# Hybrid decoder layer: key operands, head scaling and score sign between VectorE and ScalarE, and convolution steps over two PSUM banks

## The chip, the cores and the metric

One core of a Trainium2 chip runs the whole layer. The metric is the device time of one execution in microseconds; the time of the kernel before is the median of three runs, 1490.66 us (1486.98 to 1492.48). About 0.5% of it, 7.5 us, is what a measurement of this kernel can tell from no change.

## The reference, cut to what matters

One layer is computed for a prompt of 16 + 1024 rows and for 8 sample rows with a cache of 4096 past positions each. Everything is fp32.

```python
proj = rms_norm(x, ln_mix_pre) @ w_in               # q, k, v (512 each), a, g (512 each)
u = a * sigmoid(g)
s = q.k / 8 - slope[h] * (q_pos - k_pos), masked to k_pos <= q_pos   # 4 heads, 2 maps each
a = softmax(s0) - lam * softmax(s1);  o = a @ v
attn = rms_norm(o, subln) * (1 - 0.2)               # over the head's 128 values
y = causal depthwise convolution of u, width 31, + bias
conv = silu(layer_norm(y))                          # over 512 channels
x = x + rms_norm(concat(attn, conv) @ w_out, ln_mix_post)
out = x + rms_norm((silu(h @ w_gate) * (h @ w_up)) @ w_down, ln_ffn_post),  h = rms_norm(x, ln_ffn_pre)
```

## The kernel before, in words

Each fp32 matrix product on TensorE is made of three products of rounded halves (an operand's high part H in fp32r, and the rest L): H.H, H.L and L.H, in `mm3` (L146 to L149). The stages are these, in the order of the program:

- Projections. `stripe_ag(ct)` makes u for 128 channels (four of them, ct = 0 to 3), `stripe_v`, `stripe_q`, `stripe_k` make a head's values, queries and keys, each in three chunks of 280, 384 and 384 columns.
- Keys. For each chunk and each of a head's two maps `stripe_k` (L296 to L299) builds two operands of 128 partitions: R1 holds the map's 64 key rows rounded, twice (in both halves of the partitions), and R2 the remainder k - R1, twice. R1's own half is copied by ScalarE and the other by VectorE; R2's own half is subtracted by GpSimd and the other by VectorE. L1 of the queries has the rounded query in one half and its remainder in the other, so that two matmuls (L502 with R1, L503 with R2) give the scores to full precision.
- Convolution. `conv_half(ct, half)` does 31 taps over 512 columns: the first 11 go as products by ScalarE (L406, L408) and sums by GpSimd (L409) into an SBUF buffer, the other 20 by VectorE into a PSUM tile of one bank (`pcv`, two of them): L410, then L418 nineteen times, with the SBUF sum added before the last (L416). The last step writes into u. There are eight halves; their instructions are planned behind others (`high_priority(offset=-400)`).
- Attention, `attn(h, i)`: 32 units of 128 query rows, W = 144 to 1040 keys. For each map: matmuls into PSUM pieces (`ps1`), one VectorE instruction for each piece that adds the distances, scales, writes p and keeps the running maximum (L504), then for both maps the negated maximum nm (L510), the exponentials by ScalarE with their sums (L512), the factor cc (L514, L516), the combination of both maps (L520), transposes, and the product with the values (L542). After every fourth unit the head's output is scaled: copy and sums of squares by ScalarE (L550, L552), two small steps t by VectorE (L556, L557), a power by GpSimd (L559), a scaling by VectorE (L561), and two units later (`head_out`) the transposes and a copy by ScalarE (L571).
- The sample rows' attention over the cache is spread over the rest of the program by `dec_step`: the products of pages of keys with the query by GpSimd (L677, 128 of them), their sums by VectorE (L687).
- Output projection and FFN (`c_block`, `ffn`): matmuls into `ps1` tiles (mo, pg, pu, dn), emptied by VectorE and ScalarE (L907, L967, L972, L996).

Tiles of PSUM have a name and a number of buffers: `ps1` has six (`ns=6`), `pb` three, `pcv` two, `po1` and `pdec` one each. That is more than the eight banks; the framework's planner places tiles whose lives don't overlap into the same bank. It also orders each engine's instructions by a simulation of the program with its own costs, so that an edit can move instructions far from it. Each engine then runs its own list in that order. The pages' DMAs are issued from SP's queue.

Of the kernel before, what the change touches and what calls it, by code (L numbers as in the profile page):

```python
# [8 lines left out]
F32 = mybir.dt.float32  # L9
# [3 lines left out]
ALU = mybir.AluOpType  # L13
# [28 lines left out]
SLAB = 1056  # L42


@with_exitstack
def tile_layer(ctx: ExitStack, tc: tile.TileContext, I, O, cfg):
# [61 lines left out]
    subln = cst.tile([P, P], F32, name="subln")  # L108
    convb = cst.tile([P, 4], F32, name="convb")
# [174 lines left out]
    def stripe_k(h):  # L284
# [111 lines left out]
    def conv_half(ct, half):  # L396
        ut = u[ct]
        a = 512 * half
        acc = pcv(f"acc{ct}{half}")
        n = cfg["taps"]  # L400
        if n:
            if not convbuf:
                convbuf.extend(kv(f"cb{i}") for i in range(2))
            cb = convbuf[half]
            accp, t = cb[:, 0:512], cb[:, 512:1024]
            S.activation(accp, ut[:, a : a + 512], AF.Identity, scale=cw[:, ct, 0:1], bias=convb[:, ct : ct + 1])  # L406
            for k in range(1, n):
                S.mul(t, ut[:, a + k : a + k + 512], cw[:, ct, k : k + 1])  # L408
                G.tensor_tensor(accp, accp, t, op=ALU.add)  # L409
            V.tensor_scalar(acc, ut[:, a + n : a + n + 512], cw[:, ct, n : n + 1], None, op0=ALU.mult)  # L410
        else:
            V.tensor_scalar(acc, ut[:, a : a + 512], cw[:, ct, 0:1], convb[:, ct : ct + 1], op0=ALU.mult, op1=ALU.add)
        for k in range(max(n, 0) + 1, CW):
            src = ut[:, a + k : a + k + 512]
            if n and k == CW - 1:
# [65 lines left out]
    def attn(h, i):  # L481
        W = META + P * (i + 1)
        qs = slice(i * P, (i + 1) * P)
        if i == 0:
            att_st["l"] = smt(f"l{h}", 16, 2)
            att_st["ssq"] = smt(f"ssq{h}", 8, 2)
            if h == 0:
                att_st["junk"] = smt("junk", P, 1)
# [58 lines left out]
        if i % 4 == 3:  # L547
            oh = att(f"oh{h}{i}")
            b0 = i - 3
            S.copy(oh, o)  # L550
            for b in range(4):
                S.activation(att_st["junk"], oh[:, b * P : (b + 1) * P], AF.Square, accum_out=ssq[:, b0 + b : b0 + b + 1])  # L552
            bs = slice(b0, i + 1)
            l0 = lh.rearrange("p (i j) -> p i j", j=2)[:, bs, 0]
            t1 = smt(f"t1{h}{i}", 4)
# [3 lines left out]
            G.tensor_tensor(r, t1, mhalf[:, :4], op=ALU.pow)  # L559
            for b in range(4):  # L560
                V.scalar_tensor_tensor(  # L561
                    oh[:, b * P : (b + 1) * P], oh[:, b * P : (b + 1) * P], r[:, b : b + 1], subln,
                    op0=ALU.mult, op1=ALU.mult,
                )

            def head_out():
                pt = pb(f"oT{h}{i}")
                for b in range(4):
                    T.transpose(out=pt[:, b * P : (b + 1) * P], in_=oh[:, b * P : (b + 1) * P], identity=ident)
                m = att(f"mo{h}{i}")  # L570
                S.copy(m, pt)  # L571
# [697 lines left out]
    for ct in range(4):  # L1269
# [111 lines left out]
    nb=3, no=1, ns=6, nd=1, nc=2,  # L1381
# [50 lines left out]
```

## Time and profile before

| | |
|---|---|
| median of 3 runs | 1490.66 us |
| the profiled execution, its own time | 1491.31 us |
| its span | 1489.3 us |
| TensorE (PE) busy | 1375.3 us, 92% |
| VectorE (DVE) busy | 964.9 us, 65% |
| GpSimd (POOL) busy | 562.6 us, 38% |
| ScalarE (ACT) busy | 514.8 us, 35% |
| DMA | 264.35 MB, mean 178 GB/s |

The stages in the trace, in us from the span's start: the first loads to 40; projections of a and g, with the convolution beside them, to 135; attention and the remaining projections to 515, with the convolution to 227; output projection and FFN to the end. An instruction's duration on DVE includes time in which it has begun and waits for something that is not a semaphore. A busy PE is not PE at its peak, since matmuls overlap.

### The profile page before, as it was taken

The page shows a single profiled execution, that of the slowest core. Times are in us where ns is not written, and L with a number is a line of the kernel's source. Part 1 is how long each engine was busy: PE and PEld are TensorE (multiplying, and loading weights), DVE is VectorE, ACT ScalarE, POOL GpSimd, SP SyncE. Part 2 cuts the span into 40 slices and gives each one's busy share as a digit, 9 for nine tenths or more (in the row PEclk, how much of TensorE's full clock was granted, in tenths as well). Part 3 has the DMA queues.
Part 4 walks back from the last instruction along what each step waited for, and adds up shares of the span by engine and source line. Part 5 has one row for each costly group of instructions (what it writes and reads, how often), then busy time and mean ns, then how long its engine had stood idle before and what let it go on. Part 6 is the DMA issues. An engine that isn't in the chain of part 4 may idle for free.

```text
span 1489.3 us, 21639 instructions
## 1 busy us (share of the span) xinstructions
PE 1375.3 (92%) x6960; PEld 1071.5 (72%) x6960; DVE 964.9 (65%) x1531; ACT 514.8 (35%) x1021; POOL 562.6 (38%) x351
## 2 busy tenths in 40 slices
PE   6999678888875899999999999999999999999997
PEld 6999678877864778777776776767676666566666
DVE  5689998894888456855665747575654176353158
ACT  6566565547555324511312012211112112112122
POOL 3698663542425211363554445455540000000014
PEclk9999899998886899999999999999999999999999
DMA  8211012422424554768886777677676735763454
GB/s 263 72 44 45 15 44 93 121 85 92 156 81 148 181 173 136 268 214 255 278 267 208 250 244 246 235 258 267 216 253 225 260 122 192 261 192 124 162 182 173
DMA packets 199534, 264.35 MB, mean 178 GB/s; under 512 B 16279, under 2 KB 99672, under 8 KB 199413
## 3 DMA queue, kind: packets, MB, share of 16 engines
q1 hardware_dynamic: 188768, 254.40, 52.2%
q10 hardware_dynamic: 10653, 8.57, 1.8%
q8 instruction: 55, 0.90, 0.2%
q14 instruction: 58, 0.48, 0.1%
HBM read 245.92 MB, written 17.48 MB: 177 GB/s over the span
## 4 chain that ended last, share of the span: by engine, by line
PE 68%; DVE 16%; issue 5%; DMA 4%; ACT 3%; SPq 2%; POOL 1%; DVEq 0%; POOLq 0%; ACTq 0%
PE pg L147 6%; PE pg L148 6%; PE pg L149 6%; PE pu L147 5%; PE pu L148 5%; PE pu L149 5%; PE dn L147 5%; PE dn L148 5%; PE dn L149 5%; PE pv L729 4%; DVE p L504 2%; PE mo L149 2%; PE mo L147 2%; PE mo L148 2%; DVE acc L418 2%
## 5 line engine op out<-in xcount | busy, mean ns | idle before, releaser
L677 POOL TENSOR_TENSOR k<-k,qB 128x1024 f32<-128x1024 f32 x128 | 320.5, 2518 | 269.1 <-DMA k<-in_cache_k 227.6
L687 DVE TENSOR_REDUCE s<-k 128x16 f32<-128x1024 f32 x128 | 154.8, 1212 | 99.8 <-POOL k L677 95.0
L953 ACT CAST wH<-wr 128x1024 fp32r<-128x1024 f32 x66 | 69.0, 1048 | 251.9 <-DVE wL L955 148.9
L147 PE MATMUL dn<-wH,aH 128*128 128x512 f32 x352 | 141.6, 406 | 4.2 <-DVE y L996 2.6
L147 PE MATMUL pu<-hH,wH 128*128 128x512 f32 x352 | 141.0, 401 | 1.3 <-DVE y L996 1.3
L149 PE MATMUL pu<-hH,wL 128*128 128x512 f32 x352 | 139.7, 398 | 1.5 <-DVE sm2n_t L121 1.5
L148 PE MATMUL dn<-wL,aH 128*128 128x512 f32 x352 | 140.9, 400 | 0.0
L148 PE MATMUL pu<-hL,wH 128*128 128x512 f32 x352 | 140.1, 399 | 0.0
L147 PE MATMUL pg<-hH,wH 128*128 128x512 f32 x352 | 140.1, 398 | 0.0
L149 PE MATMUL dn<-wH,aL 128*128 128x512 f32 x352 | 140.0, 398 | 0.0
L148 PE MATMUL pg<-hL,wH 128*128 128x512 f32 x352 | 139.6, 396 | 0.0
L149 PE MATMUL pg<-hH,wL 128*128 128x512 f32 x352 | 139.5, 396 | 0.0
L955 DVE TENSOR_TENSOR wL<-wr,wH 128x1024 fp32r<-128x1024 f32 x66 | 104.4, 1582 | 43.8 <-ACT wH L953 23.6
L996 DVE TENSOR_TENSOR y<-dn,y 128x512 f32<-128x512 f32 x144 | 95.0, 682 | 33.7 <-PE dn L149 33.4
L409 POOL TENSOR_TENSOR cb<-cb 128x512 f32<-128x512 f32 x80 | 103.6, 1325 | 26.5 <-ACT cb L408 14.2
L418 DVE SCALAR_TENSOR_TENSOR acc<-u,cw,acc 128x512 f32<-128x512 f32 x144 | 99.5, 748 | 0.3
L1068 POOL TENSOR_TENSOR y<-y,wfpost 128x512 f32<-128x512 f32 x10 | 17.3, 1747 | 207.1 <-ACT ft L1066 207.0
L147 PEld LDWEIGHTS dn<-wH,aH 128*128 128x128 f32 x352 | 67.6, 192 | 30.7 <-issue 6.9
L147 PEld LDWEIGHTS pu<-hH,wH 128*128 128x128 f32 x352 | 66.6, 189 | 28.8 <-issue 12.0
L148 PEld LDWEIGHTS dn<-wL,aH 128*128 128x128 f32 x352 | 67.2, 191 | 24.4 <-issue 10.3
L147 PEld LDWEIGHTS pg<-hH,wH 128*128 128x128 f32 x352 | 66.2, 188 | 24.9 <-issue 9.0
L148 PEld LDWEIGHTS pu<-hL,wH 128*128 128x128 f32 x352 | 66.5, 189 | 24.2 <-issue 10.3
(582 smaller groups left out, 2986.5 us busy)
## 6 DMA issues: line engine op xcount, KB each, us to landing
k<-in_cache_k SPq DMA_DIRECT2D x256, 256.0 KB
v<-in_cache_v SPq DMA_DIRECT2D x256, 256.0 KB
wr<-in_w_gate SPq DMA_DIRECT2D x22, 512.0 KB
wr<-in_w_up SPq DMA_DIRECT2D x22, 512.0 KB
wr<-in_w_down SPq DMA_DIRECT2D x22, 512.0 KB
sd<-in_w_down SPq DMA_DIRECT2D x22, 512.0 KB
sw_gate<-in_w_gate SPq DMA_DIRECT2D x20, 512.0 KB
sw_up<-in_w_up SPq DMA_DIRECT2D x20, 512.0 KB
```

Of the source, the lines that this page charges most:

```text
L147: T.matmul(out, lhsT=wH, rhs=xH, start=first, stop=False)
L148: T.matmul(out, lhsT=wH, rhs=xL, start=False, stop=False)
L149: mark(T.matmul(out, lhsT=wL, rhs=xH, start=False, stop=last))
L409: G.tensor_tensor(accp, accp, t, op=ALU.add)
L418: V.scalar_tensor_tensor(dst, src, cw[:, ct, k : k + 1], acc, op0=ALU.mult, op1=ALU.add)
L504: V.tensor_tensor_reduce(out=p[:, a:e], in0=o, in1=bias[:, b0 + a : b0 + e], scale=SLOPES[h], scalar=NEG if a == 0 else mx[:, j : j + 1], ...
L677: x = G.tensor_tensor(kt, kt, qB.unsqueeze(1).to_broadcast([P, 2, 512]), op=ALU.mult)
L687: x = V.tensor_reduce(s.rearrange("p a c -> p (a c)"), kt.rearrange("p a (c d) -> p (a c) d", d=HD), axis=AX.X, op=ALU.add)
L729: x = T.matmul(pv[32 * g : 32 * g + 8, :], lhsT=a[:, q + i, :], rhs=vt[:, i, :], start=q + i < 4, stop=q + i >= NPG - 4, tile_position=(0, ...
L953: S.copy(H[:, :1024], raw[:, :1024])
L955: V.tensor_tensor(L[:, :1024], raw[:, :1024], H[:, :1024].bitcast(F32), op=ALU.subtract)
L996: V.tensor_tensor(y[b][:, ws], o, y[b][:, ws], op=ALU.add)
```

## The change

- In `stripe_k` the other half of R1 and the other half of R2 are copied by ScalarE (the latter from R2's own half); R2's own half stays with GpSimd.
- The scores are negated: L504 scales by the negative slope and keeps a minimum, which is nm itself; L510 is gone, and the exponential has a scale of -1.
- cc is made by `tensor_scalar` with two per-partition operands in place of `scalar_tensor_tensor`.
- A head's output: the epsilon goes in as one more column of the squares (l0 times a constant, column 129 of each block in a tile of its own tag, `oh`), so that t is gone; the scaling by r is done by ScalarE, and subln is applied with a per-partition factor (`sublnT`, a new DMA of 128 values and one ScalarE step at the start) in the copy after the transposes.
- The convolution runs over 1024 columns in one PSUM tile of two banks, one buffer; ScalarE's first step covers 1024 columns, the other products and sums stay at 512, in two halves of one buffer.
- `ns` goes from 6 to 4.

```diff
+    sublnT = cst.tile([P, 1], F32, name="sublnT")
...
                 S.copy(R1s[j][sl, d], k[sl, d])
-                V.tensor_copy(R1s[j][ot, d], k[sl, d])
-                (G if cfg["r2_g"] else V).tensor_tensor(R2s[j][sl, d], k[sl, d], R1s[j][sl, d].bitcast(F32), op=ALU.subtract)
-                V.tensor_tensor(R2s[j][ot, d], k[sl, d], R1s[j][sl, d].bitcast(F32), op=ALU.subtract)
+                S.copy(R1s[j][ot, d], k[sl, d])
+                G.tensor_tensor(R2s[j][sl, d], k[sl, d], R1s[j][sl, d].bitcast(F32), op=ALU.subtract)
+                S.copy(R2s[j][ot, d], R2s[j][sl, d].bitcast(F32))
...
+            D.dma_start(sublnT, I["subln_w"][0].rearrange("(p o) -> p o", o=1))
+        S.mul(sublnT, sublnT, (1.0 - LAM_INIT) * P ** 0.5)
...
+        acc = ps.tile([P, SEQ], F32, tag="c", name=f"acc{ct}", bufs=1)
...
+        S.activation(accp, ut[:, 0:SEQ], AF.Identity, scale=w(0), bias=convb[:, ct : ct + 1])
+        for k in range(1, n):
+            for a in (0, 512):
+                S.mul(t[:, a : a + 512], ut[:, a + k : a + k + 512], w(k))
+            for a in (0, 512):
+                G.tensor_tensor(accp[:, a : a + 512], accp[:, a : a + 512], t[:, a : a + 512], op=ALU.add)
+        V.tensor_scalar(acc, ut[:, n : n + SEQ], w(n), None, op0=ALU.mult)
+        for k in range(n + 1, CW):
+            src = ut[:, k : k + SEQ]
+            if k == CW - 1:
                 V.tensor_tensor(acc, acc, accp, op=ALU.add)
+            V.scalar_tensor_tensor(acc if k < CW - 1 else src, src, w(k), acc, op0=ALU.mult, op1=ALU.add)
...
-                    out=p[:, a:e], in0=o, in1=bias[:, b0 + a : b0 + e], scale=SLOPES[h],
-                    scalar=NEG if a == 0 else mx[:, j : j + 1], op0=ALU.add, op1=ALU.max, accum_out=mx[:, j : j + 1],
+                    out=p[:, a:e], in0=o, in1=bias[:, b0 + a : b0 + e], scale=-SLOPES[h],
+                    scalar=-NEG if a == 0 else nm[:, j : j + 1], op0=ALU.add, op1=ALU.min, accum_out=nm[:, j : j + 1],
...
-        V.tensor_scalar(nm, mx, -1.0, None, op0=ALU.mult)
...
-        V.scalar_tensor_tensor(cc, lh[:, 2 * i : 2 * i + 1], neglam, rl, op0=ALU.mult, op1=ALU.mult)
+        V.tensor_scalar(cc, lh[:, 2 * i : 2 * i + 1], neglam, rl, op0=ALU.mult, op1=ALU.mult)
...
-            V.scalar_tensor_tensor(t1, l0, EPS, l0, op0=ALU.mult, op1=ALU.mult)
-            V.scalar_tensor_tensor(t1, ssq[:, bs], 1.0 / P, t1, op0=ALU.mult, op1=ALU.add)
+            S.mul(ov[:, :, P], l0, (P * EPS) ** 0.5)
+            for b in range(4):
+                S.activation(att_st["junk"], ov[:, b, : P + 1], AF.Square, accum_out=ssq[:, b0 + b : b0 + b + 1])
...
-                V.scalar_tensor_tensor(
-                    oh[:, b * P : (b + 1) * P], oh[:, b * P : (b + 1) * P], r[:, b : b + 1], subln,
-                    op0=ALU.mult, op1=ALU.mult,
-                )
+                S.mul(ov[:, b, :P], ov[:, b, :P], r[:, b : b + 1])
...
-                S.copy(m, pt)
+                S.mul(m, pt, sublnT)
...
-    nb=3, no=1, ns=6, nd=1, nc=2,
+    nb=3, no=1, ns=4, nd=1, nc=2,
```

## Rows read from the trace of the kernel before

**Rows 1.** The page's first part: busy us, share of the span, instructions
```profile
PE 1375.3 (92%) x6960; PEld 1071.5 (72%) x6960; DVE 964.9 (65%) x1531; ACT 514.8 (35%) x1021; POOL 562.6 (38%) x351
```

**Rows 2.** Stretches: PE, PEld, DVE, ACT, POOL busy (count), granted clock, DMA share, GB/s
```profile
40.00:135.00 95.00, 95.00 (x601) 92.94 (x601) 77.74 (x125) 55.44 (x89) 73.21 (x59) 1.00 0.13 38
135.00:240.00 105.00, 81.82 (x473) 76.87 (x472) 102.41 (x192) 60.07 (x132) 64.40 (x47) 0.89 0.16 48
240.00:320.00 80.00, 72.16 (x486) 68.15 (x485) 70.01 (x161) 49.37 (x142) 35.72 (x25) 1.00 0.32 97
320.00:400.00 80.00, 62.90 (x392) 59.82 (x391) 56.46 (x103) 48.41 (x112) 30.69 (x18) 0.85 0.40 129
400.00:515.00 115.00, 84.85 (x461) 73.29 (x461) 85.59 (x202) 56.24 (x146) 47.23 (x28) 0.81 0.38 125
515.00:1489.00 974.00, 952.12 (x4400) 675.29 (x4398) 550.81 (x695) 217.62 (x356) 294.50 (x146) 0.99 0.66 218
```

**Rows 3.** The chain of waits from 135 to 515 us, shares by engine and line
```profile
by line: issue 11.5%; DVE p L504 8.2%; DVE acc L418 7.8%; DVE p L520 6.1%; DVE R L299 5.0%; DVE R L297 4.4%; PE o L542 3.9%; ACT p L512 3.7%; DVE cc L516 3.4%; DVE oh L561 2.4%; DVE nm L510 2.4%; DVE s L687 2.2%; PE AT L528 1.9%; DVE L L268
```

**Rows 4.** Groups of DVE from 135 to 515: count, busy us, mean ns, idle before
```profile
L418 DVE SCALAR_TENSOR_TENSOR acc<-u,cw,acc 128x512 f32<-128x512 f32 x59 | 42.0, 745 | 0.2
...
L299 DVE TENSOR_TENSOR R<-kT,R 64x384 fp32r<-64x384 f32 (+1 forms) x24 | 22.7, 946 | 0.7
L516 DVE SCALAR_TENSOR_TENSOR cc<-l,neglam,rl 128x1 f32<-128x1 f32 x32 | 20.2, 631 | 0.3
L297 DVE CAST R<-kT 64x384 fp32r<-64x384 f32 (+1 forms) x24 | 19.5, 817 | 0.6
L561 DVE SCALAR_TENSOR_TENSOR oh<-oh,or,subln 128x128 f32<-128x128 f32 x32 | 16.7, 583 | 2.4 <-POOL or L559 2.3
L510 DVE TENSOR_SCALAR nm<-mx 128x2 f32<-128x2 f32 x32 | 16.7, 525 | 0.3
L557 DVE SCALAR_TENSOR_TENSOR t<-ssq,t 128x4 f32<-128x4 f32 x8 | 5.4, 674 | 12.9 <-ACT junk L552 12.9
L556 DVE SCALAR_TENSOR_TENSOR t<-l 128x4 f32<-128x4 f32 x8 | 4.5, 558 | 2.6 <-ACT p L512 2.6
```

**Rows 5.** Single lines of the kernel: duration ns min/median/max, first and last start
```profile
L510 DVE TENSOR_SCALAR nm<-mx x32: 149/170/2379, 166.9 to 476.7; 128x2 f32<-128x2 f32 x32
...
L121 DVE TENSOR_SCALAR hr_t<-hs x8: 135/154/155, 515.9 to 603.2; 128x1 f32<-128x1 f32 x8
```

**Rows 6.** Timeline of DVE and POOL in the last head: start us, us, what
```profile
460.88 2.36 POOL L138 TENSOR_TENSOR wo3L<-wo3r,wo3H 128x1024 fp32r<-128x1024 f32 x1 [1.82 <-ACT wo3H L136]
461.09 2.17 DVE L516 SCALAR_TENSOR_TENSOR cc<-l,neglam,rl 128x1 f32<-128x1 f32 x1
...
463.29 1.03 DVE L520 SCALAR_TENSOR_TENSOR p<-p,cc,p 128x400 f32<-128x400 f32 x2
```

**Rows 7.** Timeline of three convolution steps, then DVE's 1024-column step of L911
```profile
192.49 2.06 DVE L418 SCALAR_TENSOR_TENSOR acc<-u,cw,acc 128x512 f32<-128x512 f32 x3
...
L911 DVE SCALAR_TENSOR_TENSOR xr<-z,zr_r,xr x8: 1278/1284/1286, 513.4 to 597.9; 128x1024 f32<-128x1024 f32 x8
```

**Rows 8.** Groups of ACT from 135 to 515
```profile
L296 ACT CAST R<-kT 64x384 fp32r<-64x384 f32 (+1 forms) x24 | 11.3, 480 | 0.5
...
L436 ACT ACTIVATE u<-yT,ln2n,ln_r 128x128 f32<-128x128 f32 x4 | 1.7, 467 | 6.7 <-DVE ln2n L427 6.7
```

**Rows 9.** Who waited for whom: us in total, times, longest; 110 to 515, then 515 on
```profile
ACT p L512 <- DVE nm L510: 43.4, 20, 9.4
...
POOL k L677 <- DMA k<-in_cache_k: 26.5, 2, 21.1
...
DVE s L687 <- POOL k L677: 90.7, 35, 6.6
...
DVE s L709 <- POOL dg L704: 40.6, 7, 7.0
```

**Rows 10.** The page's group of L996: count, busy us, mean ns, idle before
```profile
L996 DVE TENSOR_TENSOR y<-dn,y 128x512 f32<-128x512 f32 x144 | 95.0, 682 | 33.7 <-PE dn L149 33.4
```

More of the change, by code (lines that the diff above doesn't have):

```diff
@@ L42 @@
 SLAB = 1056
+OHW = P + 4
 @with_exitstack
@@ L368, in att_consts @@
         V.tensor_scalar(subln, subln, 1.0 - LAM_INIT, None, op0=ALU.mult)
+        with nc.allow_non_contiguous_dma("128 values, once"):
+            D.dma_start(sublnT, I["subln_w"][0].rearrange("(p o) -> p o", o=1))
+        S.mul(sublnT, sublnT, (1.0 - LAM_INIT) * P ** 0.5)
         D.dma_start(pts, I["page_table"].rearrange("(o b) n -> o (b n)", o=1))
@@ L394, in tile_layer, with conv @@
     convbuf = []
-    def conv_half(ct, half):
+    def conv(ct):
         ut = u[ct]
-        a = 512 * half
-        acc = pcv(f"acc{ct}{half}")
+        acc = ps.tile([P, SEQ], F32, tag="c", name=f"acc{ct}", bufs=1)
         n = cfg["taps"]
[L401 to L415, printed above, removed]
+        if not convbuf:
+            convbuf.extend(kv(f"cb{i}") for i in range(2))
+        accp, t = convbuf
+        w = lambda k: cw[:, ct, k : k + 1]
+        S.activation(accp, ut[:, 0:SEQ], AF.Identity, scale=w(0), bias=convb[:, ct : ct + 1])
[8 more added lines that the diff above has]
+            if k == CW - 1:
                 V.tensor_tensor(acc, acc, accp, op=ALU.add)
-            dst = acc if k < CW - 1 else src
-            V.scalar_tensor_tensor(dst, src, cw[:, ct, k : k + 1], acc, op0=ALU.mult, op1=ALU.add)
+            V.scalar_tensor_tensor(acc if k < CW - 1 else src, src, w(k), acc, op0=ALU.mult, op1=ALU.add)
     def ln_stats(src, rows, name):
@@ L487, in attn @@
             if h == 0:
-                att_st["junk"] = smt("junk", P, 1)
+                att_st["junk"] = smt("junk", P + 1, 1)
         lh, ssq = att_st["l"], att_st["ssq"]
@@ L495, in attn @@
         pj = []
-        mx = smt(f"mx{h}{i}", 2, 4)
+        nm = smt(f"nm{h}{i}", 2, 4)
         for j in range(2):
@@ L504, in attn @@
                 V.tensor_tensor_reduce(
-                    out=p[:, a:e], in0=o, in1=bias[:, b0 + a : b0 + e], scale=SLOPES[h],
-                    scalar=NEG if a == 0 else mx[:, j : j + 1], op0=ALU.add, op1=ALU.max, accum_out=mx[:, j : j + 1],
+                    out=p[:, a:e], in0=o, in1=bias[:, b0 + a : b0 + e], scale=-SLOPES[h],
+                    scalar=-NEG if a == 0 else nm[:, j : j + 1], op0=ALU.add, op1=ALU.min, accum_out=nm[:, j : j + 1],
                 )
             pj.append(p)
-        nm = smt(f"nm{h}{i}", 2, 4)
-        V.tensor_scalar(nm, mx, -1.0, None, op0=ALU.mult)
         for j in range(2):
-            S.activation(pj[j][:, :W], pj[j][:, :W], AF.Exp, bias=nm[:, j : j + 1], accum_out=lh[:, 2 * i + j : 2 * i + j + 1])
+            S.activation(
+                pj[j][:, :W], pj[j][:, :W], AF.Exp, scale=-1.0, bias=nm[:, j : j + 1],
+                accum_out=lh[:, 2 * i + j : 2 * i + j + 1],
+            )
+        cc = smt(f"cc{h}{i}", 1, 4)
         rl = smt(f"rl{h}{i}", 1, 4)
         V.reciprocal(rl, lh[:, 2 * i + 1 : 2 * i + 2])
-        cc = smt(f"cc{h}{i}", 1, 4)
-        V.scalar_tensor_tensor(cc, lh[:, 2 * i : 2 * i + 1], neglam, rl, op0=ALU.mult, op1=ALU.mult)
+        V.tensor_scalar(cc, lh[:, 2 * i : 2 * i + 1], neglam, rl, op0=ALU.mult, op1=ALU.mult)
         A = pj[0]
@@ L547, in attn @@
         if i % 4 == 3:
-            oh = att(f"oh{h}{i}")
+            oh = at.tile([P, 4 * OHW], F32, tag="oh", name=f"oh{h}{i}", bufs=2)
+            ov = oh.rearrange("p (b e) -> p b e", e=OHW)
             b0 = i - 3
-            S.copy(oh, o)
-            for b in range(4):
-                S.activation(att_st["junk"], oh[:, b * P : (b + 1) * P], AF.Square, accum_out=ssq[:, b0 + b : b0 + b + 1])
+            S.copy(ov[:, :, :P], o.rearrange("p (b e) -> p b e", e=P))
             bs = slice(b0, i + 1)
             l0 = lh.rearrange("p (i j) -> p i j", j=2)[:, bs, 0]
-            t1 = smt(f"t1{h}{i}", 4)
-            V.scalar_tensor_tensor(t1, l0, EPS, l0, op0=ALU.mult, op1=ALU.mult)
-            V.scalar_tensor_tensor(t1, ssq[:, bs], 1.0 / P, t1, op0=ALU.mult, op1=ALU.add)
+            S.mul(ov[:, :, P], l0, (P * EPS) ** 0.5)
+            for b in range(4):
+                S.activation(att_st["junk"], ov[:, b, : P + 1], AF.Square, accum_out=ssq[:, b0 + b : b0 + b + 1])
             r = smt(f"or{h}{i}", 4)
-            G.tensor_tensor(r, t1, mhalf[:, :4], op=ALU.pow)
+            G.tensor_tensor(r, ssq[:, bs], mhalf[:, :4], op=ALU.pow)
             for b in range(4):
-                V.scalar_tensor_tensor(
-                    oh[:, b * P : (b + 1) * P], oh[:, b * P : (b + 1) * P], r[:, b : b + 1], subln,
-                    op0=ALU.mult, op1=ALU.mult,
-                )
+                S.mul(ov[:, b, :P], ov[:, b, :P], r[:, b : b + 1])
             def head_out():
@@ L568, in head_out @@
                 for b in range(4):
-                    T.transpose(out=pt[:, b * P : (b + 1) * P], in_=oh[:, b * P : (b + 1) * P], identity=ident)
+                    T.transpose(out=pt[:, b * P : (b + 1) * P], in_=ov[:, b, :P], identity=ident)
                 m = att(f"mo{h}{i}")
-                S.copy(m, pt)
+                S.mul(m, pt, sublnT)
                 if h < NH - 1:
@@ L1278, in tile_layer @@
         with tc.high_priority(offset=-cfg["conv"]):
-            conv_half(ct, 1)
-            conv_half(ct, 0)
+            conv(ct)
     att_fixed()
```

## The prediction

> **What bounds the kernel now.** I read the busy shares first, then a table by stretch, then the chain of waits of the stretch that is not full. The shares [rows 1] say PE, at 92%; the table [rows 2] says where it is not so. From 40 to 135 us PE is busy in all of 95 us, and from 515 to the end in 952.1 of 974. Between 135 and 515 it is busy in 81.8 + 72.2 + 62.9 + 84.9 = 301.8 of 380 us: 78 us idle, at a granted clock of 0.89, 1.00, 0.85 and 0.81, so part of the busy time too ran at 1.2 instead of 2.4 GHz. In that stretch DVE is busy in 102.4 + 70.0 + 56.5 + 85.6 = 314.5 us, and in its first 105 us in 102.4. The chain there [rows 3] names it: L504, L418, L520, L299, L297, cc, oh and nm, all on DVE. So attention is bound by DVE, with waits from instruction to instruction, and the FFN by PE. The edits take work from DVE in attention alone, except that the FFN loses two PSUM buffers.
>
> One thing must be seen before the terms are added up. nm is a step over 128x2 values; its median is 170 ns and its longest 2379 [rows 5]. The timeline shows of cc, which is as small, how that comes [rows 6]: the cc of 461.09 ends at 463.26, 20 ns after the POOL instruction that began before it (460.88 + 2.36 = 463.24). Such DVE steps stand until POOL's SBUF instruction is done, and their durations hold that wait.
>
> **DVE's side, from 135 to 515** [rows 4].
> - Keys: L297 (24 x 817 ns = 19.5) and L299 (24 x 946 ns = 22.7) leave: 42.2 us.
> - nm, 32 x 525 ns: 16.7 us leave.
> - t, 5.4 + 4.5: 9.9 us leave.
> - The heads' scaling L561, 32 x 583 ns: 16.7 us leave.
> - cc stays as `tensor_scalar` over 128x1, for which L121 has 135 to 155 ns in all of eight [rows 5], so 4.8 us remain of 20.2. But in most units L520 follows at once and needs SBUF too: at 461.09 it would have met the same POOL instruction as cc did. The gain lies between 0 (every wait moves to L520) and 15.4 (none does); I take 5, nearer to the pattern in the timeline.
> - Convolution: three dense steps take 2.06 us, the last with its tail, and with the mean of 0.745 [rows 4] their pitch is (2.06 - 0.745) / 2 = 0.66 [rows 7]. A step of 1024 columns in two PSUM banks isn't in the trace. L911's 1284 ns is the nearest row; less the 745 - 660 = 85 ns by which such steps overlap it is 1.20 us a step against 2 x 0.66 = 1.32. The bounds are 0.66 us saved (a second 512 columns for nothing) and 0.66 lost (the step takes three times as long as one half, if the second bank is dear); I take 0.12, by L911. After 135 us there are 59 steps in the row [rows 4], 30 pairs: 4 us, with bounds from -20 to 20. What lies before 135 is under a full PE and counts for nothing.
>
> Sum: 42.2 + 16.7 + 9.9 + 16.7 + 5 + 4 = 94.5 of 314.5 us.
>
> The Trainium skill (SBUF — State Buffer, Who interferes with whom) has a rule that bears on cc: it counts `tensor_scalar` among the forms that can take the port pair shared with GpSimd for the whole instruction. By it cc would go on waiting and its term would be 0 instead of 5. The row of 128x2 (up to 2379 ns) agrees with the rule, that of 128x1 (at most 155) doesn't; 5 us don't decide the forecast.
>
> **ACT's side.** It gains 48 copies of keys at L296's mean, 48 x 0.48 = 23.0 us, 32 scalings of 128x128 at L436's 0.467 (which has two operands beside the data, so an upper end): 15.0, and eight small steps for the epsilon column, at the same price 3.7 [rows 8]: 42 us. The eight copies that get a factor stay where they are. It was busy in 60.1 + 49.4 + 48.4 + 56.2 = 214 of 380 us [rows 2] and will be in 256. That is below PE's 302, so the cover holds in the mean; from 240 to 400 it is 98 of 160 before and, with half of the 42, some 119 after, of a shorter stretch, and there ACT is late next. Two new waits stand in ACT's list: the copy of R2's other half waits for POOL's subtraction, and the scaling of the heads for POOL's power. Behind them are exponentials and the copies out of the transposes, for which PE waits. POOL's list has L677 in it, which once waited 21.1 us for a page [rows 9].
>
> The Trainium skill (ScalarE: Activation LUTs, Rules for kernel authors) speaks against this move: copies and products belong to VectorE, up to about three times as fast per element in bf16. An estimate by that factor: the 48 key steps would cost DVE a third of ACT's 23.0 us, 7.7, and DVE's sum would be 60 us instead of 94.5. Here DVE's key steps average 817 and 946 ns [rows 4] and ACT's copy of the same size 480 [rows 8], because DVE's hold the waits for POOL: the rule loses.
>
> **From DVE's time to the end.** The chain tells how much of this was on the path. Of 380 us it has 5.0 + 4.4% for the keys, 2.4% for nm and 2.4% for oh, 14.2% or 54 us; convolution's saving there is 0.12 / 1.32 of 7.8%, 3 us; t has no share in the row as printed, and I count half of its 9.9: 62 us is the ceiling. Against it stand, on the same path, the key copies by ACT (24 more in R1 and 24 in R2, half of them behind others: 12 us) and the heads' tail on ACT (8 x 1 us): 42 us. And PE's order takes its turn: 78 us of idle time can't all go, since each unit still has its scores, minimum, exponential and transposes one after the other in the last head. I take 30 us for attention, between 10 (the waits for POOL fall on L520 and on POOL itself) and 60. PE's clock is in it: denser work keeps the upper level longer, as in 240:320.
>
> **The FFN with four `ps1` buffers.** A dn tile is six matmuls at 952 / 4400 = 0.22 us, 1.3 us. With six buffers DVE may be five tiles late, 6.5 us, before PE stands; with four, three tiles, 3.9. After 515 us DVE stood 35 + 7 = 42 times for POOL, 131 us in all, 3.1 in the mean and 7.0 at most [rows 9]; only the longest of them outlast four buffers. If a fifth of them, eight, cost 0.7 us each, that is 5 to 6 us; I take 5, with 0 and 30 as ends (all 42 at 0.7).
>
> The sum against the profiled execution: 1491.3 - 30 + 5 = 1466 us; its span of 1489.3 and 2.0 us around it stand 0.65 us above the median of the runs, which is nothing here. The other edits (a DMA of 128 values, one ACT step at the start) lie under the full PE at 50 us.
>
> **The rivals.**
> - *A larger gain.* Every wait removed was on the path and the clock stays up: the ceiling of 62 less 5, below 1436. For it: DVE at 102.4 of 105 us from 135 on. Against it: the last head's units wait in turn.
> - *ACT's list gives it back.* The R2 copies stand behind POOL: 24 of them, half a page product each (1.2 us), 29 us, against the gain of 30, and the time is 1491, no change. For it: L677 in POOL's list, the 21.1 us wait. Against it: the scores waited for POOL's half of R2 before as well.
> - *Slower: the down projection is short of buffers.* dn tiles come every 1.3 us and DVE needs 0.68 for one [rows 10], so a delay is made up slowly, and each of the 42 stands can cost PE its length beyond 3.9 us and some of what follows. At 1 us each it is 42 us against 30, 1503. It decides from 0.7 us each on; with attention at its lower end (10) from 0.25 us. For it: DVE is the only engine that empties dn. Against it: DVE has 551 of 974 us of work there [rows 2], and L996 itself waited 33 us for PE [rows 10], so it is often ahead.
> - *It does not do what it says.* A 1024-column step costs as much as two: 4 us of the sum, 1470; that is inside the forecast.
>
> **How the numbers follow.** Forecast, 1436 to 1481: 0.65. The larger gain, under 1436: 0.07. ACT gives it back, 1483 to 1498: 0.13. Slower, over 1498: 0.15. Faster by over 0.5% (under 1483) 0.72, within 0.13, slower 0.15. The range leaves out the larger gain and about four fifths of the slower case, 0.19: 1436 to 1500.
>
> **What would show it.** Right: from 135 us on PE's idle time falls from 78 to about 45, DVE's busy time there by 80 or more, attention ends near 485 instead of 515; L297, L299, L510, L556, L557 and L561 are gone from DVE; ACT's wait for nm (43.4 us) [rows 9] is smaller; the convolution's step takes about 1.28 us; cc never lasts over 0.2 us and L520's mean is longer. The FFN's PE idle time grows from 22 us by about 5. Wrong: the attention stage as long as before with ACT waiting for POOL in the key copies; or the same 30 us gained there and PE waiting for L996 in the FFN by as much; or a convolution step over 1.5 us.

## The result and the profile after

The changed kernel takes 1453.68 us (median of 4 runs, 1452.15 to 1454.12) where the kernel before, run beside it, takes 1488.82 (1485.22 to 1492.48): a ratio of 0.9762, 95% interval 0.9734 to 0.979. It is 35 us faster; the forecast was 25 us, to 1466, with a range of 1436 to 1500.

The page's first part answers to [rows 1]: DVE has lost 100 us of work and ACT has gained 38.

```profile
PE 1357.4 (93%) x6960; PEld 1055.7 (73%) x6960; DVE 864.6 (60%) x1319; ACT 552.6 (38%) x1110; POOL 556.5 (38%) x351
```

To divide the time I use an event that every version has: the first matmul of the output projection (tile mo). It needs three heads and the first four units of the last one. The rest of the last head ends soon after it: its last transposes start 11.4 to 13.3 us after mo in all fourteen kernels, so the cut falls at the same place in each. The first mo starts at 498.1 us before and at 453.3 after. The table by stretch of the kernel before, cut there (columns as in [rows 2]):

```profile
135.00:498.10 363.10, 284.83 (x1724) 265.06 (x1722) 307.91 (x641) 208.51 (x513) 174.11 (x114) 0.87 0.30 96
498.10:1489.30 991.20, 969.01 (x4484) 688.35 (x4483) 557.37 (x709) 223.21 (x373) 298.44 (x149) 0.99 0.66 217
```

And after, first in the stretches of [rows 2], then cut at its own mo:

```profile
40.00:135.00 95.00, 93.54 (x586) 91.09 (x586) 73.66 (x76) 52.78 (x81) 70.17 (x55) 1.00 0.16 45
135.00:240.00 105.00, 94.24 (x592) 90.75 (x590) 88.85 (x156) 83.39 (x188) 73.82 (x56) 0.93 0.20 63
240.00:320.00 80.00, 71.45 (x478) 68.15 (x477) 57.12 (x132) 64.08 (x166) 35.91 (x25) 0.96 0.34 106
320.00:400.00 80.00, 71.61 (x470) 67.14 (x469) 44.51 (x111) 67.64 (x163) 40.42 (x24) 0.96 0.47 154
...
135.00:453.30 318.30, 268.92 (x1744) 254.09 (x1743) 225.62 (x486) 247.98 (x605) 177.13 (x118) 0.93 0.34 109
453.30:1451.90 998.60, 968.36 (x4477) 685.38 (x4475) 544.50 (x705) 224.87 (x377) 293.10 (x149) 0.99 0.65 215
```

The reader is to see three things. Attention is 44.8 us shorter, and the rest 7.4 us longer (998.6 against 991.2); the difference is the whole change of the span, 37.4 us (the medians differ by 35.1; the profiled execution of the kernel before was slower than its median). The 44.8 are 28.9 us of PE's idle time (363.1 - 284.8 = 78.3 before, 318.3 - 268.9 = 49.4 after) and 15.9 us of PE's busy time, although 20 matmuls more fall into the stretch (1744 against 1724): the granted clock rose from 0.87 to 0.93, that is, less of the stretch was spent at 1.2 GHz. And DVE, busy in 102.4 of the first 105 us before, is no longer the fullest engine: with 225.6 us it now stands behind PE (268.9) and ACT (248.0).

DVE's groups from 135 to 475 us after (columns as in [rows 4]). The lines of keys, nm, t and the heads' scaling are gone; L420 is the convolution's step of 1024 columns, L519 is cc:

```profile
L523 DVE SCALAR_TENSOR_TENSOR p<-p,cc,p 128x400 f32<-128x400 f32 (+7 forms) x52 | 45.8, 913 | 0.5
L420 DVE SCALAR_TENSOR_TENSOR acc<-u,cw,acc 128x1024 f32<-128x1024 f32 x32 | 41.0, 1282 | 0.4
...
L519 DVE TENSOR_SCALAR cc<-l,neglam,rl 128x1 f32<-128x1 f32 x32 | 8.5, 268 | 0.5
```

ACT's groups of the same stretch. L299 and L301 replace DVE's copy and subtraction; they take ACT 480 ns each where DVE's steps took 817 and 946 [rows 4]:

```profile
L299 ACT CAST R<-kT 64x384 fp32r<-64x384 f32 (+1 forms) x24 | 11.5, 480 | 0.6
L301 ACT CAST R<-R 64x384 fp32r<-64x384 f32 (+1 forms) x24 | 11.5, 481 | 0.5
L298 ACT CAST R<-kT 64x384 fp32r<-64x384 f32 (+1 forms) x24 | 11.5, 477 | 0.4
...
L563 ACT ACTIVATE oh<-oh,or 128x128 f32<-128x128 f32 x32 | 10.2, 392 | 12.6 <-POOL or L561 12.6
```

The waits of that stretch (us in total, times, longest). The wait of ACT for nm, 43.4 us before [rows 9], is 10.3; DVE now waits for ACT's exponentials (41.1 us, 15.8 before), and PE for the heads' tail on ACT (15.7 us; before, 7.4 for the same tail on DVE):

```profile
DVE rl L518 <- ACT p L512: 41.1, 16, 10.4
...
PE oT L568 <- ACT oh L563: 15.7, 3, 12.3
ACT oh L563 <- POOL or L561: 12.6, 4, 8.5
...
ACT p L512 <- DVE nm L506: 10.3, 12, 2.6
```

PE's waits from mo to the end, before:

```profile
PE pv L729 <- DMA v<-in_cache_v: 5.0, 3, 3.7
PE dn L147 <- DVE y L996: 2.6, 2, 2.0
...
PE pu L149 <- DVE sm2n_t L121: 1.5, 1, 1.5
...
PE pu L147 <- DVE y L996: 1.3, 1, 1.3
```

and after, where L996 has become L995:

```profile
PE pv L728 <- DMA v<-in_cache_v: 10.6, 6, 4.8
PE pu L151 <- DVE sm2n_t L123: 4.0, 1, 4.0
...
PE dn L149 <- DVE y L995: 1.3, 1, 1.3
PE pu L151 <- DVE wL L954: 1.3, 1, 1.3
PE dn L150 <- DVE wL L954: 0.8, 1, 0.8
```

All the waits listed for PE there come to 13.8 us before and 21.9 after, and its idle time to 22.2 and 30.2, so the list accounts for the 8 us that PE idles more: pages of values 5.6, DVE's L123 (L121 before) 2.5 and its splitting of weights (L954, which is L955 before) 2.1, less 2.6 at L996 (at dn and pu together, 3.9 before and 1.3 after).

### The profile page after: what moved, and what is told of

Read it like the earlier page. It is cut to its first block, busy times and chain, and to the rows that moved or that the text cites. A ratio compares the mean times of both kernels' runs of the same rounds, so it can differ in the third digit from the quotient of the medians.

```text
span 1451.9 us, 21493 instructions
## 1 busy us (share of the span) xinstructions
PE 1357.4 (93%) x6960; PEld 1055.7 (73%) x6960; DVE 864.6 (60%) x1319; ACT 552.6 (38%) x1110; POOL 556.5 (38%) x351
## 4 chain that ended last, share of the span: by engine, by line
PE 50%; DMA 5%; SPq 5%; DVE 5%; issue 4%; POOL 2%; ACT 0%; DVEq 0%; POOLq 0%; ACTq 0%
PE pu L149 5%; PE pu L151 5%; PE pu L150 5%; PE pg L149 5%; PE pg L150 4%; PE pg L151 4%; PE dn L149 3%; PE pv L728 3%; PE dn L151 3%; PE dn L150 3%; SPq L662 2%; DMA k<-in_cache_k 2%; SPq L656 2%; PE mo L149 2%; PE mo L151 2%
## 5 line engine op out<-in xcount | busy, mean ns | idle before, releaser
L954 DVE TENSOR_TENSOR wL<-wr,wH 128x1024 fp32r<-128x1024 f32 x66 | 97.5, 1479 | 49.4 <-ACT wH L952 21.7
L995 DVE TENSOR_TENSOR y<-dn,y 128x512 f32<-128x512 f32 x144 | 94.8, 684 | 41.1 <-PE dn L151 40.7
L414 POOL TENSOR_TENSOR cb<-cb,cb 128x512 f32<-128x512 f32 x80 | 102.2, 1308 | 20.3 <-ACT cb L412 10.5
L149 PEld LDWEIGHTS dn<-wH,aH 128*128 128x128 f32 x352 | 66.8, 190 | 43.4 <-issue 13.2
L978 ACT CAST aH<-sg 128x512 fp32r<-128x512 f32 x44 | 27.3, 621 | 180.0 <-DVE sg L971 179.9
L1067 POOL TENSOR_TENSOR y<-y,wfpost 128x512 f32<-128x512 f32 x10 | 14.3, 1437 | 210.4 <-ACT ft L1065 210.2
L420 DVE SCALAR_TENSOR_TENSOR acc<-u,cw,acc 128x1024 f32<-128x1024 f32 x72 | 92.6, 1285 | 1.6
L151 PEld LDWEIGHTS pu<-hH,wL 128*128 128x128 f32 x352 | 66.5, 189 | 26.8 <-DVE wL L954 6.1
L149 PEld LDWEIGHTS pg<-hH,wH 128*128 128x128 f32 x352 | 66.1, 188 | 25.7 <-issue 9.0
```

Of the source, the lines that this page charges most:

```text
L149: T.matmul(out, lhsT=wH, rhs=xH, start=first, stop=False)
L151: mark(T.matmul(out, lhsT=wL, rhs=xH, start=False, stop=last))
L414: G.tensor_tensor(accp[:, a : a + 512], accp[:, a : a + 512], t[:, a : a + 512], op=ALU.add)
L420: V.scalar_tensor_tensor(acc if k < CW - 1 else src, src, w(k), acc, op0=ALU.mult, op1=ALU.add)
L954: V.tensor_tensor(L[:, :1024], raw[:, :1024], H[:, :1024].bitcast(F32), op=ALU.subtract)
L995: V.tensor_tensor(y[b][:, ws], o, y[b][:, ws], op=ALU.add)
```

## The experiments

My theory: the keys' steps on DVE, long because they stand for POOL, bound attention, and the four `ps1` buffers take a little back in the FFN. The rivals: another edit made the gain; what helped was only a new order of the instructions; the loss after attention has nothing to do with the buffers. The kernels ran in three groups of four, each group beside runs of the kernel before (medians 1487.18, 1488.93 and 1487.59 us). The numbers of all, from the results and from tables by stretch cut at mo (times are medians of several runs, the last four columns come from one execution each):

| kernel | time us | ratio [95%] | mo starts | mo to end | DVE busy, 135 to mo | ACT busy |
|---|---|---|---|---|---|---|
| before | 1488.82 | | 498.1 | 991.2 | 307.9 | 208.5 |
| after | 1453.68 | 0.9762 [0.9734, 0.979] | 453.3 | 998.6 | 225.6 | 248.0 |
| keys alone | 1448.08 | 0.9752 [0.9734, 0.9771] | 460.9 | 984.2 | 260.1 | 237.1 |
| negated scores alone | 1472.62 | 0.9894 [0.9876, 0.9912] | 476.2 | 995.7 | 293.4 | 208.1 |
| heads alone | 1483.97 | 0.9972 [0.9957, 0.9988] | 486.1 | 999.5 | 294.6 | 214.9 |
| convolution, four buffers | 1490.4 | 1.001 [0.9995, 1.0025] | 491.0 | 998.0 | 297.2 | 209.0 |
| after, six buffers | 1441.64 | 0.9682 [0.9658, 0.9707] | 449.3 | 990.0 | 223.0 | 249.8 |
| before, four buffers | 1494.06 | 1.0031 [1.0011, 1.0051] | 495.5 | 997.0 | 301.4 | 209.8 |
| nm in two steps | 1491.64 | 1.0017 [0.9999, 1.0034] | 495.3 | 993.6 | 303.4 | 214.6 |
| cc alone | 1481.04 | 0.9946 [0.9928, 0.9964] | 492.7 | 988.5 | 301.9 | 205.7 |
| keys, DVE's time put back | 1476.31 | 0.9917 [0.9899, 0.9936] | 483.2 | 994.2 | 285.8 | 228.9 |
| R1 alone | 1467.67 | 0.9866 [0.9846, 0.9885] | 475.9 | 989.1 | 285.6 | 216.2 |
| after, keys back on DVE | 1474.03 | 0.9902 [0.9886, 0.9919] | 481.4 | 991.7 | 268.2 | 227.4 |
| after, without convolution, six buffers | 1444.15 | 0.9709 [0.9692, 0.9725] | 450.5 | 991.0 | 229.7 | 245.6 |

**Keys alone.**

```diff
-                V.tensor_copy(R1s[j][ot, d], k[sl, d])
...
-                V.tensor_tensor(R2s[j][ot, d], k[sl, d], R1s[j][sl, d].bitcast(F32), op=ALU.subtract)
+                S.copy(R1s[j][ot, d], k[sl, d])
...
+                S.copy(R2s[j][ot, d], R2s[j][sl, d].bitcast(F32))
```

> Before, with the key operands' edit alone (both copies by ScalarE). Theory (VectorE's steps and their stands beside GpSimd bound attention): VectorE loses about 42 us of busy time before the output projection, the output projection's first matmul comes 15 to 20 us earlier than before's 498, the time is about 1474. Rival (the planner's new order, not VectorE's time, made the gain): the time moves by under 7 us, in either direction, or by as much as the whole change. Rival (ScalarE's list gives it back behind GpSimd's subtraction): VectorE loses the 42 us but the output projection starts at 498 as before, 1489.

It takes 1448.08 us, 39 less than before beside it: more than twice what I expected, and as much as the whole change. That was also a sign that I had given to the planner's new order, so this run alone does not decide between the two; the test that puts DVE's time back does. Its stretches, cut at mo:

```profile
135.00:460.90 325.90, 274.59 (x1744) 257.57 (x1742) 260.11 (x596) 237.09 (x568) 174.51 (x116) 0.91 0.32 105
460.90:1445.11 984.21, 962.36 (x4477) 684.35 (x4475) 548.35 (x709) 223.56 (x373) 296.60 (x149) 0.99 0.66 219
```

Of the 498.1 - 460.9 = 37.2 us at mo, DVE's 47.8 us less of work are the likely source. The chain had given the keys 9.4% of 380 us, 36 us [rows 3], and that is what came.

**Negated scores alone.**

```diff
-        V.tensor_scalar(nm, mx, -1.0, None, op0=ALU.mult)
-            S.activation(pj[j][:, :W], pj[j][:, :W], AF.Exp, bias=nm[:, j : j + 1], accum_out=lh[:, 2 * i + j : 2 * i + j + 1])
+            S.activation(pj[j][:, :W], pj[j][:, :W], AF.Exp, scale=-1.0, bias=nm[:, j : j + 1], accum_out=lh[:, 2 * i + j : 2 * i + j + 1])
```

(with L504 scaled by the negative slope and keeping a minimum, as in the change)

> Before, with the negated scores alone (no step for the negated maximum). Theory: ScalarE's wait for that step (43.4 us) falls to under 20, VectorE loses 16.7 us, the output projection starts 8 to 12 us earlier, about 1480. Rival (the stand moves to the next VectorE step with two SBUF inputs, the combination L520): L520's 40.8 us grow by 10 or more and the time stays within 4 us of 1489.

It takes 1472.62 us. The gain at mo is 21.9 us, more than the 8 to 12 expected, and more than the 14.5 us by which DVE's time fell, so DVE's time is not all of it; what else is in it I did not separate. ACT's wait for the maximum did not shrink:

```profile
ACT p L510 <- DVE nm L504: 41.9, 23, 5.3
```

So the small step itself was not what ACT had waited for; I read the wait as one for DVE to come round to the unit at all. In the five kernels in which both key copies are on ACT this wait is 10.3 to 28.2 us, in the nine others 36.8 to 56.9.

**Heads alone** (the diff of `attn` and `head_out` without the rest).

> Before, with the heads' scaling alone (epsilon as a column, scaling by ScalarE, subln in the copy). Theory: VectorE loses 26.6 us, ScalarE gains about 20 with its wait for GpSimd's power, the output projection starts about 5 us earlier, 1484. Rival (ScalarE gives it back): no earlier start, 1489 or more.

1483.97 us is the time expected, but by two misses that cancel: mo comes 12.0 us earlier instead of 5, and 8.3 us of it are lost again after mo. A gain of 0.28% is also less than what can be told from no change. Of the 26.6 us that leave DVE, its busy time shows only 13.3, and its groups tell where some of the rest is: the combination of both maps has become the costliest group. Before:

```profile
L520 DVE SCALAR_TENSOR_TENSOR p<-p,cc,p 128x400 f32<-128x400 f32 (+7 forms) x52 | 40.8, 816 | 0.5
```

and with the heads alone:

```profile
L525 DVE SCALAR_TENSOR_TENSOR p<-p,cc,p 128x400 f32<-128x400 f32 (+7 forms) x52 | 52.6, 1040 | 0.7
...
L515 DVE TENSOR_SCALAR nm<-mx 128x2 f32<-128x2 f32 x32 | 20.0, 625 | 0.4
```

The same instructions take 11.8 us more, and nm 3.3 more than in [rows 4]; cc takes 5.9 less (14.3).

**Convolution alone, with four buffers** (the diff of `conv_half`, and `ns` = 4).

> Before, with the convolution over 1024 columns in two banks, and the four PSUM buffers that it needs to be placed. Theory: a step takes 1.28 us, VectorE loses about 11 us over the convolution, of which 4 after 135 us; the time is 1485 to 1491. Rival (the four buffers cost the down projection 5 us or more): the output projection starts 3 us earlier and the rest takes 5 us more than 991.

1490.4 us, no change, with a step of 1290 ns (median of 72). As the rival had it, mo comes earlier (7.1 us) and the rest takes more (6.8). What a dense sequence shows is said at the end.

**The changed kernel with six buffers.**

```diff
-    nb=3, no=1, ns=4, nd=1, nc=2,
+    nb=3, no=1, ns=6, nd=1, nc=2,
```

> The changed kernel with six buffers instead of four. Two causes for the 7 us that the changed kernel loses after the output projection's first matmul (998.6 us against 991.2). Theory (it is the order in which cached pages arrive: TensorE waited 10.6 us for pages of values, before 5.0): six buffers change nothing there, the rest takes 995 to 1000 us, the time is 1450 to 1457. Rival (four buffers, as the prediction had it): the rest takes 991 us and the time is about 1446.

**The kernel before with four buffers** (the same edit the other way round).

> Before, with four buffers instead of six and nothing else. Theory (buffers aren't short): within 5 us of before, and TensorE's wait for L996 in the FFN stays under 5 us. Rival (four buffers cost the down projection): the rest after the output projection's start takes 5 us or more above 991, with TensorE waiting for L996, 1494 or more.

The first gives 1441.64 us, the fastest version of this study; its interval [0.9658, 0.9707] lies below that of the change [0.9734, 0.979]. The second gives 1494.06, slower by 0.31%, less than can be told from no change. From mo to the end the first takes 8.6 us less than the changed kernel, the second 5.8 more than before. In the changed kernel with six buffers:

```profile
135.00:449.30 314.30, 266.04 (x1753) 253.17 (x1751) 223.04 (x486) 249.82 (x608) 176.86 (x119) 0.94 0.34 109
449.30:1439.30 990.00, 965.92 (x4472) 686.33 (x4472) 545.76 (x704) 224.23 (x376) 295.04 (x149) 0.99 0.65 217
```

In the kernel before with four:

```profile
495.50:1492.51 997.01, 968.13 (x4474) 686.49 (x4473) 545.05 (x710) 223.53 (x373) 293.72 (x149) 0.99 0.65 216
```

So in both pairs the rest is 6 to 9 us longer with four buffers, as the rivals had it. Why, they had wrong: PE does not lose the time waiting for the down projection's buffers. Its waits with six buffers in the changed kernel, from mo on:

```profile
PE pv L728 <- DMA v<-in_cache_v: 7.8, 5, 3.7
PE pu L151 <- DVE sm2n_t L123: 2.3, 1, 2.3
PE dn L149 <- DVE y L995: 2.2, 1, 2.2
```

and with four in the kernel before:

```profile
PE pv L729 <- DMA v<-in_cache_v: 11.4, 6, 4.4
...
PE pu L149 <- DVE wL L955: 4.7, 2, 3.3
...
PE dn L148 <- DVE wL L955: 0.8, 1, 0.8
```

With four buffers the waits for pages of values are longer (10.6 and 11.4 us, against 7.8 and 5.0), and the wait for L996 is no longer. In the kernel before, pages (6.4 us more with four buffers) and L955 (5.5 more), less L996 (3.9) and L121 (1.5), make up nearly all of the 6.7 us by which PE idles more after mo. That the number of buffers makes pages late is not shown: each edit also makes the planner find a new order, and heads alone, with six buffers, waits 9.1 us for pages and has a rest of 999.5, while the changed kernel with the keys back, with four, waits 6.4 and has 991.7. The line of heads alone:

```profile
PE pv L730 <- DMA v<-in_cache_v: 9.1, 4, 4.5
```

**nm in two steps.** nm is made in two steps over 128x1 in place of one over 128x2, so that it does not stand for POOL (the cc's form had suggested it).

```diff
-        V.tensor_scalar(nm, mx, -1.0, None, op0=ALU.mult)
+        for j in range(2):
+            V.tensor_scalar(nm[:, j : j + 1], mx[:, j : j + 1], -1.0, None, op0=ALU.mult)
```

> Before, with the negated maximum made by two steps over 128x1 in place of one over 128x2: one VectorE instruction more in each of 32 units, none of them of a form that was seen to stand for GpSimd. Theory (the stands are the cost): no such step lasts over 0.2 us, ScalarE's wait for them (43.4 us) falls, the combination L520 grows by some of what is gone, the output projection starts 5 to 12 us earlier, 1477 to 1484. Rival (the number of steps in the chain is the cost, as the gain of the negated scores alone, 14.6 us, could also be read): the same as before or slower, 1489 to 1492.

The line shows that no step stands any more (min, median, max ns):

```profile
L511 DVE TENSOR_SCALAR nm<-mx x64: 128/146/154, 159.1 to 475.2; 128x1 f32<-128x1 f32 x64
```

Yet the time is unchanged, 1491.64 us, and the groups of other steps have become dearer:

```profile
L299 DVE TENSOR_TENSOR R<-kT,R 64x384 fp32r<-64x384 f32 (+1 forms) x24 | 24.7, 1030 | 0.7
...
L562 DVE SCALAR_TENSOR_TENSOR oh<-oh,or,subln 128x128 f32<-128x128 f32 x32 | 21.7, 737 | 5.3 <-POOL or L560 5.3
```

L299 went from 22.7 to 24.7 us, the heads' scaling from 16.7 to 21.7 [rows 4] and L520 from 40.8 to 43.2: part of the stand taken from one step is met by others that need SBUF. L297 and cc became cheaper (15.3 and 17.4 us). nm itself takes 8.9 us instead of 16.7, DVE in all 4.5 less; mo comes 2.8 us earlier, and the rest takes 2.4 more. ACT's wait for nm stays (43.6 us). So the theory's 5 to 12 us did not come, and the time is the rival's. This run does not refute that the number of steps counts; cc alone, next, speaks against it, since it gains with as many steps as before.

**cc alone.**

```diff
-        V.scalar_tensor_tensor(cc, lh[:, 2 * i : 2 * i + 1], neglam, rl, op0=ALU.mult, op1=ALU.mult)
+        V.tensor_scalar(cc, lh[:, 2 * i : 2 * i + 1], neglam, rl, op0=ALU.mult, op1=ALU.mult)
```

> Before, with cc as tensor_scalar alone. Theory: the 32 steps fall from 20.2 to about 8.5 us and L520 grows by about half of the difference, since it meets the same GpSimd instruction; 2 to 6 us faster, 1483 to 1487. Rival (all of the stand moves to L520): L520 grows by 11 us, the time stays within 2 us.

1481.04 us, 0.54% faster, a little more than expected; mo comes 5.4 us earlier for 6.0 us less of DVE. DVE's groups in it show cc falling from 20.2 to 8.6 us. L520 takes 2.0 of the 11.6 back (40.8 us before), not half, and L299 takes 3.9 (22.7 before):

```profile
L520 DVE SCALAR_TENSOR_TENSOR p<-p,cc,p 128x400 f32<-128x400 f32 (+7 forms) x52 | 42.8, 851 | 0.4
...
L299 DVE TENSOR_TENSOR R<-kT,R 64x384 fp32r<-64x384 f32 (+1 forms) x24 | 26.6, 1113 | 0.6
...
L516 DVE TENSOR_SCALAR cc<-l,neglam,rl 128x1 f32<-128x1 f32 x32 | 8.6, 270 | 0.5
```

**Keys on ACT, and DVE's time put back.** With the key copies on ACT, for each of the 24 pairs of copies two sums over the same data are added on DVE; they are used by nothing.

```diff
+                dj = smt(f"dj{h}{c}{j}", 1, 4)
+                for _ in range(2):
+                    V.tensor_reduce(dj[sl], k[sl, d], axis=AX.X, op=ALU.add)
```

> The key operands' edit alone (e1), and 48 sums by VectorE over 64x384 or 64x272 of the key tile into a value that nobody reads: one SBUF input each, so by the rows they don't stand for GpSimd. They put back some 26 us of VectorE time at the places where the edit took 42 away. Theory (VectorE's time until the output projection sets its start; over the runs so far 47.8 us less gave 37.2 us earlier, 0.78 for one): the start moves from 460.9 back to 475 to 485, the time to 1462 to 1472. Rival (it was only the stands beside GpSimd, or the planner's new order): it stays within 5 us of 461 and 1448.

The sums never stand (404 to 551 ns):

```profile
L302 DVE TENSOR_REDUCE dj<-kT x48: 404/539/551, 151.8 to 399.5; 64x1 f32<-64x384 f32 x32, 64x1 f32<-64x272 f32 x16
```

DVE's busy time rises by 25.7 us and mo by 22.3, to 483.2, as expected for it (475 to 485); the time, 1476.31, is above what I expected, since the rest is 994.2 instead of 984.2 us. This is the sharpest of the tests. ACT still makes the key copies, so neither a quicker way to R1 and R2 nor the absence of stands is what counts: DVE's occupied time in this place is, stands or not, at 0.87 us of the stage for each us of DVE. The sums bring a new order too, but 22.3 us is twice what any kernel here lies off the common line (11 us, below), and it came as forecast.

**R1 alone.** Only the copy of R1's other half goes to ACT.

```diff
-                V.tensor_copy(R1s[j][ot, d], k[sl, d])
+                S.copy(R1s[j][ot, d], k[sl, d])
```

> Before, with only the first of the two key copies (R1's other half, L297's 19.5 us) given to ScalarE; the subtraction L299 stays with VectorE. Theory (VectorE's time): 308 less 19.5 is about 288 us from 135 on, the start is near 483, the time about 1473. Rival (the subtraction with its two SBUF inputs is what mattered): under 5 us gained, 1484 or more.

1467.67 us, somewhat better than the 1473 expected: 22.2 us earlier at mo for 22.3 us of DVE, more than half of what both copies give. R2's copy, which waits on ACT for POOL, adds the other 15.0 (475.9 to 460.9).

**The changed kernel with the keys back on DVE.** `stripe_k` is that of before, all else as in the change.

> The changed kernel (four buffers) with the key operands as before (two steps by VectorE). Theory (VectorE's time): 225.6 + 42 = 268 us, the output projection starts at 465 to 470, the time is 1463 to 1470: the keys are worth 10 to 16 us beside the other edits where alone they gave 39. Rival (the keys alone made the gain, the others cancel): 1480 or more.

1474.03 us, against 1463 to 1470 expected, and mo starts at 481.4, not at 465 to 470: a miss. DVE's 268.2 us are as forecast, but keys alone, with 260.1, starts mo 20.5 us earlier. So the total of DVE's time does not set the start by itself; the keys' steps weigh more than others of the same length. They are worth 20 us of the time beside the other edits (28.1 at mo, for 42.6 us of DVE), and 39 alone.

**The changed kernel without the convolution's edit, with six buffers.**

> The changed kernel without the convolution's edit: six buffers, two accumulators of one bank; keys, negated scores, cc and heads as changed. Theory (the convolution gives little beside the others, and the four buffers cost 6 to 9 us): within 6 us of the changed kernel with six buffers, 1437 to 1449, faster than the changed kernel. Rival (the convolution's 1024 columns are worth their 11 us beside the others): 1450 or more.

1444.15 us. Its interval, 0.9692 to 0.9725, overlaps with that of the changed kernel with six buffers: the 1024-column steps give at most a few us here, less than the 12 us between the changed kernels with six and with four buffers.

## Why the prediction was right, and where not

The mechanism held. DVE bounded attention; it lost 82 us there (94.5 summed); L297, L299, L510, L556, L557 and L561 are gone; PE's idle time from 135 us on fell from 78 to 49 (45 forecast); ACT's wait for nm shrank, though not because the step is gone (41.9 us with the negated scores alone, 20.0 with the keys alone). The putting back of DVE's time shows, for the keys, the cause and not only the coincidence.

**The attention term was too small: 30 us, measured 44.8.** The ceiling of 62 us, read from the chain, was sounder than what I set against it. I had taken off 12 us for ACT's key copies and 8 for the heads' tail, and then 12 more for PE's turn. The first hardly appeared: with the keys alone PE waited 3.8 us for L297's copy by ACT, and the chain's 36 us for the keys came as 37.2. The tail did appear in the changed kernel (PE waited 15.7 us for ACT's oh, 12.3 at once), and attention gained 44.8 all the same. And the clock, which I had named in this term, had no number of its own: 15.9 of the 44.8 us are busy time saved at 0.93 instead of 0.87.

**The FFN term had the right size and the wrong place: 5 us, measured 7.4.** I worked it out from DVE's lateness in emptying dn, and expected PE to wait for L996. Both pairs of kernels that differ in the buffers alone agree with the size (8.6 and 5.8 us after mo), but PE's wait for L996 at dn went from 2.6 to 1.3 us. The longer waits are those for pages of values and for single DVE steps, and what makes them longer stays open. That step of the working is refuted; the number came out near by chance.

**The terms of the sum.** Keys 42.2 us: DVE's work fell by 47.8 with the keys alone. nm 16.7: 14.5. t and heads, 26.6: 13.3 with the heads alone, where L520 and nm grew. Convolution 4: with and without it, at six buffers, DVE has 223.0 and 229.7 us, but mo starts at 449.3 and 450.5, and the dense pace did not change (last section). cc 5: 6.0. For cc I had 4.8 us left of 20.2 by L121's 155 ns, a step whose two scalars are constants; cc's are read per partition, and it is 8.5, at 268 ns, so the sign "never over 0.2 us" failed, while the other sign, a longer L520 (40.8 to 45.8 us), came. The timeline of DVE after shows that wait at its new place (the second of the two L523 steps begins at 419.57, just after POOL's, and lasts 2.69 us):

```profile
418.39 0.27 DVE L519 TENSOR_SCALAR cc<-l,neglam,rl 128x1 f32<-128x1 f32 x1
418.69 3.57 DVE L523 SCALAR_TENSOR_TENSOR p<-p,cc,p 128x400 f32<-128x400 f32 x2
```

and that of POOL, whose instruction of 419.19 ends at 421.85 while L523 is still under way:

```profile
419.19 2.66 POOL L676 TENSOR_TENSOR k<-k,qB 128x1024 f32<-128x1024 f32 x1
```

**The sum was not the gain.** Alone, the edits bring mo forward by 37.2, 21.9, 12.0, 7.1 and 5.4 us, 83.6 together, and in one kernel 44.8. Keys and negated scores alone make 59. Once DVE is at 260 us of a stage of 326, PE (275) and ACT (237) are nearly as full, and what else is taken from DVE is worth less: from the keys alone to the changed kernel with six buffers DVE loses 37.1 us more and mo comes 11.6 earlier. A straight line through the fourteen kernels (mo against DVE's busy time) has 0.55 us for each us of DVE, with kernels up to 11 us off it. The order, which every edit changes, may be part of that scatter; I did not separate it. The rest after mo goes from 984.2 to 999.5 us with no simple reason, and some of the gain of the keys alone (7.0 us of its 39) is such a difference.

**The rivals.** ACT's list did not give it back: the R2 copies behind POOL were worth 15.0 us in favour. The down projection did not run short: its wait for L996 fell. The larger gain, below 1436, was not reached, but the version with six buffers, at 1441.64, came near to it. The convolution's step as dear as two is what happened, and it cost next to nothing, as that rival said.

## What to carry to other kernels

Where one engine bounds a stage, put a price on its large steps by the chain's share, and take little off it for waits on the engine that receives the work unless that engine is itself nearly full; then add what the clock gives back. Here that price was right for the keys (36 us, and 37.2 came) and wrong for small steps (nm 9 us, and 21.9 came; cc 13, and 5.4 came). Stop counting when the next engine is as full: here the keys alone did what all the edits together did, and the edit that came with a price (two buffers for wider steps that gave at most a few us) was better left out. To test whether an engine's time is the cause, put useless time of the same length back in its place.

## What the runs showed of the hardware

- A DVE step of one column per partition in the form `tensor_scalar` did not stand for POOL in any of 64 cases (at most 154 ns, though 21 of them began while a POOL instruction was under way), nor did cc in that form (242 to 276 ns, x32), where nm over two columns took up to 2379 ns [rows 5] and cc as `scalar_tensor_tensor` 631 in the mean [rows 4]. The Trainium skill (SBUF — State Buffer, Who interferes with whom) counts `tensor_scalar` among the forms that can take the ports shared with GpSimd when their operands meet certain conditions; the row over two columns agrees, and no step over one column was seen to wait for them.
- cc, a step over 128x1 with two operands read per partition, took 268 ns, where L121, of the same form and size with two constants, took 135 to 155 [rows 5].
- In a dense sequence the step of 1024 columns over two PSUM banks has the same pace as two of 512: six in 7.91 us after, 1.32 each, and ten in 6.68 us before, 0.67 each. Neither a cost of the second bank nor a gain from the saved instruction shows in it.

The timeline of the convolution after:

```profile
107.73 7.91 DVE L420 SCALAR_TENSOR_TENSOR acc<-u,cw,acc 128x1024 f32<-128x1024 f32 x6
```

and before:

```profile
106.21 6.68 DVE L418 SCALAR_TENSOR_TENSOR acc<-u,cw,acc 128x512 f32<-128x512 f32 x10
```

- ACT's copies of the keys vary by about 2% at most at either size (64x384: 509 to 514 ns, 64x272: 410 to 419), those of DVE six- and sevenfold (352 to 2521 and 296 to 1848). The line of ACT's L299 after (min, median, max ns), and that of DVE's L297 before, which it replaces:

```profile
L299 ACT CAST R<-kT x24: 410/512/514, 152.6 to 384.1; 64x384 fp32r<-64x384 f32 x16, 64x272 fp32r<-64x272 f32 x8
```

```profile
L297 DVE CAST R<-kT x24: 296/791/2521, 150.9 to 412.3; 64x384 fp32r<-64x384 f32 x16, 64x272 fp32r<-64x272 f32 x8
```

The Trainium skill (ScalarE: Activation LUTs, Rules for kernel authors) gives products and sums to VectorE, as the faster engine per element (copies it does not name). DVE's quickest copy agrees, at 296 ns against 410 on ACT; its mean, 817 ns against 480, does not, and the move to ACT gave 39 us.
